# A recurrence's triangular inverse: substitution in 16-blocks, and one more block step on TensorE

## The chip, the cores and the metric

The program runs on one core of a Trainium2 chip. The core has five engines with queues of their own: TensorE (PE, matmuls), VectorE (DVE), ScalarE (ACT), GpSimd (POOL) and SyncE (SP, which here only issues DMAs). Each takes its instructions in the order written, and waits on semaphores for what it needs from the others. The metric is the device time of one execution in microseconds: 2445.03 us before, the median of 3 runs (2442.17 to 2445.43).

## The reference

Two layers of a diffusion backbone over 512 latent and 256 context tokens of width 1024. In each, three token mixers read one normalised input: a bidirectional RWKV-7 recurrence, a latent attention (MLA) and a windowed attention (GQA); their gated outputs are merged and projected. The change touches the recurrence alone:

```python
def step(S, inp):
    r_t, w_t, k_t, v_t, kk_t, a_t = inp
    sa = jnp.einsum('bhvk,bhk->bhv', S, kk_t)
    S = (S * w_t[:, :, None, :] - sa[..., None] * (kk_t * a_t)[:, :, None, :]
         + v_t[..., None] * k_t[:, :, None, :])
    return S, jnp.einsum('bhvk,bhk->bhv', S, r_t)
```

It runs over 768 steps for 8 heads of 64 channels, once in each direction, and all in float32.

## The kernel before, in words

The recurrence is not run step by step but in 12 chunks of 64 steps (`NCH`). Inside a chunk the steps depend on each other through a strictly triangular 64 x 64 matrix, one for each of the 16 pairs of head and direction; the kernel inverts one plus that matrix once and then needs matmuls alone. `zphase` computes the matrices on PE and leaves them in device memory (`tt_d`). `rwkv` works through the chunks: `rwkv_scores` loads a chunk's operands two chunks ahead and makes its score products (tiles `scps`, `AR`, `TR`, `bkp`), and `rwkv_step` makes the chunk's own chain: `Rp` (state and scores), `Up` (the inverse in `YB` times Rp), `Sp` (the new state `So`), and `Yp` (the output).

Inverses are made for four chunks at a time (`NS`, `NG` = 3 groups a layer), so there are six in the program. `rwkv_inverse` holds 64 matrices, in two 32 x 32 diagonal blocks each and one block off the diagonal. A 32-row strip of the 128 partitions holds one row of every block of its kind. The two kinds of diagonal blocks are inverted on DVE by substitution: for j from 30 to 1, a product of a column of the matrix and a row of the inverse (L630, j(31 - j) elements a partition), added to the rows above (L632). Three 32 x 32 transposes on DVE (L620 in front; L635 and L636 behind) turn the blocks as they are needed, and POOL's `affine_select` (L624) makes the start values. The block off the diagonal is then two matmul products on PE, `zp` (L645) and `yp` (L653), each in two halves of 16 matrices; these matmuls take 32 rows and 32 columns of the array, on two of its four strips in turn. ACT and DVE copy the results into `YB` (L648, L654, L655).

What sets the order. `band(b)` gives instructions a rank, and a scheduler fills each engine's queue by rank where dependencies allow it. The recurrence has rank `B + 1`. Fill work, the input projections that the attentions will need (tiles `g`, `st`; `wh` and `wl` are the high and low part of a weight, split by ACT in L165 and POOL in L166), has rank `B + 4`. `pace(n)` puts n steps of fill work there; a step is six matmuls in layer 0 (three over 512 columns and three over 256) and mostly three over 512 columns in layer 1. `in_line` adds an order for PE: every matmul of the recurrence from the end of the first inverse's substitution on is tied behind the one written before it. The fill between them counts too. So PE runs them exactly as written, and a matmul that waits holds all that follow.

```python
ahead = invert(0)
for _ in range(3):
    next(ahead)
...
pace(FILL[l][1])
...
    for _ in ahead:
        pace(FILL[l][2])
```

A generator's `yield` marks where the caller goes on with something else. The first inverse of a layer is driven by the lines above: substitution, `FILL[l][1]` steps of fill, then products with `FILL[l][2]` steps between. The inverses of the next groups are driven from the chunk loop, one `next(ahead)` behind each of the first three chunks of a group and up to three within the fourth; there the fill steps are `FILL[l][3]` and `FILL[l][4]`, 2 or 3 behind each part of a chunk.

Of the kernel before, what the change touches and what calls it, by code (L numbers as in the profile page):

```python
# [10 lines left out]
F32 = mybir.dt.float32  # L11
F32R = mybir.dt.float32r
BF16 = mybir.dt.bfloat16
AF = mybir.ActivationFunctionType
ALU = mybir.AluOpType
# [4 lines left out]
P = 128  # L20
# [9 lines left out]
GB, RB, CB = 2, 3, 2  # L30


FILL = ((48, 36, 2, (2, 2, 2), (3, 3, 3), 2), (72, 56, 4, (2, 2, 2), (3, 3, 3), 2))

QUEUES = (("scalar", "sync", "sync", "scalar"), ("sync", "scalar", "sync", "sync"))

# [1 line left out]
NS, NG = 4, 3  # L38
# [22 lines left out]
def build(tc, A, out):  # L61
    nc = tc.nc
    V, S, G, TE, DMA = nc.vector, nc.scalar, nc.gpsimd, nc.tensor, nc.sync
    weights = {}
    es = ExitStack()
    cpool = es.enter_context(tc.tile_pool(name="const", bufs=1))
# [3 lines left out]
    rps = es.enter_context(tc.tile_pool(name="rps", bufs=2, space=PSUM))  # L70
# [4 lines left out]
    @contextmanager  # L75
    def band(b):

        keep, mine = tc.cur_priority, bands.get(b, b * 1000000)
        tc.cur_priority = mine
        yield  # L80
        bands[b] = tc.cur_priority
        tc.cur_priority = keep
# [12 lines left out]
            DMA.dma_start(xs[k], A["xT"][:, k, :])  # L95
    C = {n: cst[:, o:o + w] for n, (o, w) in CC.items() if o < n_cst}
    ident, bones, ones = C["ident"], C["bones"], C["ones"]
    kbias = cpool.tile([P, 3], F32, name="kbias")
    V.memset(kbias[:, 0:1], EPS)
    V.memset(kbias[:, 1:2], GN_EPS)  # L100
    V.memset(kbias[:, 2:3], 10.0 * math.log(2.0))
    b_eps, b_gn, b_kk = kbias[:, 0:1], kbias[:, 1:2], kbias[:, 2:3]


# [35 lines left out]
    def queued(i):  # L140

        if line["on"] and line["last"] is not None:
            tc.add_manual_dep(i.ins, line["last"].name, mybir.DependencyInfo(
                mybir.DependencyClass.NoSync, mybir.DependencyReason.DATA), reason="line")
        line["last"] = i.ins

    @contextmanager
    def in_line():
        line["on"] = True
        yield  # L150
        line["on"] = False

    def mm(o, l, r, start=True, stop=True, **kw):
        queued(TE.matmul(o, l, r, start=start, stop=stop, **kw))  # L154
# [309 lines left out]
    def rwkv(l, D, last, DL, B, pace, zlast):  # L464

        with tc.tile_pool(name="rw", bufs=1, reuse_waits="tile") as rp:
            yo = rp.tile([P, 4, T], F32, name="yo")
            st = {"seen": set(), "S": None}
            parts, YB = {}, {}

            def scores(i):
                if i < NCH:
                    parts[i] = yield from rwkv_scores(l, last, rp, i)

            def invert(g):
                if g < NG:
                    YB[g] = rp.tile([P, 32, 64], F32, tag="YB", name="YB", bufs=2)
                    yield from rwkv_inverse(l, rp, g, YB[g])

            def rest(*gens):  # L480
                for g in gens:
                    for _ in g:
                        pass

            with band(B + 1):
                rest(scores(0), scores(1))
                ahead = invert(0)
                for _ in range(3):
                    next(ahead)
            with band(B + 4), tc.issue_after(zlast):  # L490
                pace(FILL[l][1])
            with band(B + 1), in_line():
                for _ in ahead:
                    pace(FILL[l][2])
                ahead = out = iter(())
                for i in range(NCH):
                    if i % NS == 0:
                        rest(ahead)
                        ahead = invert(i // NS + 1)
                    nxt = scores(i + 2)  # L500
                    step = rwkv_step(l, last, i, yo, st, DL, rp, parts.pop(i), YB[i // NS])
                    for n in FILL[l][3 if i % NS < NS - 1 else 4]:
                        next(step, None)
                        next(nxt, None)
                        if i % NS == NS - 1:
                            next(ahead, None)
                        next(out, None)
                        pace(n)
                    rest(step, nxt)
                    if i % NS < NS - 1:  # L510
                        next(ahead, None)
                    if i in READY and (i > 3 or not last):
                        rest(out)
                        out = readout(l, D, rp, yo, READY[i])
                for _ in out:
                    pace(FILL[l][5])

# [89 lines left out]

    def rwkv_inverse(l, rp, g, YB):

        TT = rp.tile([P, 8, NS, 64], F32, tag="TT", name="TT")  # L610
        cs = slice(g * NS, (g + 1) * NS)
        for b0 in (0, 64):

            DMA.dma_start(TT[b0:b0 + 32], tt_d[l][b0:b0 + 32, :, cs])
            DMA.dma_start(TT[b0 + 32:b0 + 64, :, :, 0:32], tt_d[l][b0 + 32:b0 + 64, :, cs, 32:64])
        inv = rp.tile([P, 1536], F32, tag="inv", name="inv")
        MB, tmp = inv[:, 0:1024], inv[:, 1024:1536]
        YK = YB[:, :, 32:64]
        TT4 = TT.rearrange("p c s t -> p (c s) t")
        V.transpose(MB, TT4[:, :, 0:32].rearrange("p n j -> p j n"))  # L620

        M3 = MB.rearrange("p (j i) -> p i j", i=32)
        Y3 = YK.rearrange("p j i -> p i j")
        G.affine_select(YK, MB.rearrange("p (j i) -> p j i", i=32),  # L624
                        [[1, 32], [-1, 32]], ALU.is_gt, 0.0, base=0, channel_multiplier=0)
        V.memset(YB.rearrange("p n c -> p (n c)")[:, 32:2048:65], 1.0)
        for j in range(30, 0, -1):
            n = 31 - j
            t3 = tmp[:, 256 * (j % 2):256 * (j % 2) + j * n].rearrange("p (i c) -> p i c", c=n)
            V.tensor_tensor(t3, M3[:, 0:j, j:j + 1].to_broadcast([P, j, n]),  # L630
                            Y3[:, j:j + 1, j + 1:32].to_broadcast([P, j, n]), ALU.mult)
            V.tensor_tensor(Y3[:, 0:j, j + 1:32], Y3[:, 0:j, j + 1:32], t3, ALU.add)  # L632
            if j in (22, 12):
                yield
        V.transpose(YB[:, :, 0:32].rearrange("p n j -> p j n"), YK)  # L635
        V.transpose(MB.rearrange("p (n j) -> p n j", j=32), YB[:, :, 0:32])  # L636
        for b0 in (32, 96):
            S.copy(YB[b0:b0 + 32, :, 32:64], YB[b0:b0 + 32, :, 0:32])
        X13 = MB.rearrange("p (n j) -> p n j", j=32)
        yield  # L640
        for n0 in range(0, 32, 16):
            zp = rps.tile([P, 16, 32], F32, tag="r", name="zp", bufs=RB)
            for n in range(16):
                for b0 in (0, 64):
                    mm(zp[b0 + 32:b0 + 64, n, :], TT4[b0:b0 + 32, n0 + n, 32:64], X13[b0:b0 + 32, n0 + n, :])  # L645
            z3 = tmp.rearrange("p (n j) -> p n j", j=32)
            for b0 in (32, 96):
                S.copy(z3[b0:b0 + 32], zp[b0:b0 + 32])  # L648
            yield
            yp = rps.tile([P, 16, 32], F32, tag="r", name="yp", bufs=RB)  # L650
            for n in range(16):
                for b0 in (0, 64):
                    mm(yp[b0:b0 + 32, n, :], z3[b0 + 32:b0 + 64, n, :], YB[b0 + 32:b0 + 64, n0 + n, 32:64])  # L653
            S.copy(YB[0:32, n0:n0 + 16, 32:64], yp[0:32])  # L654
            V.tensor_copy(YB[64:96, n0:n0 + 16, 32:64], yp[64:96])  # L655
        for b0 in (32, 96):
            G.memset(YB[b0:b0 + 32, :, 0:32], 0.0)
# [726 lines left out]
    for l in range(2):  # L1384
# [41 lines left out]
        def pace(n):  # L1426

            for _ in zip(range(n), steps):
                pass
# [3 lines left out]
        with band(B + 4):  # L1433
            pace(FILL[l][0])
        ss = cpool.tile([P, 6, 10], F32, tag="ss", name="ss")
        if last:
            cctx.close()
            with band(B + 3):
                gqa_tokens(l, F, last, ss)
        rwkv(l, D, last, DL, B, pace, zlast)  # L1440
        weights["queue"] = getattr(nc, QUEUES[l][2])
        with band(B + 4), tc.issue_after(line["last"]):
            pace(22 * 8 - sum(FILL[l][0:2]) - 2 * FILL[l][2] - NG * (3 * sum(FILL[l][3]) + sum(FILL[l][4])) - 4 * FILL[l][5])

        def gates():
            with band(B + 4):
# [160 lines left out]
```

## Time and profile before

| | before |
|---|---|
| median of 3 runs | 2445.03 us (2442.17 to 2445.43) |
| the profiled execution | 2438.52 us, span 2436.8 us |
| mean granted clock of PE | 0.947 |
| PE busy | 2190.0 us, 90% of the span |
| PE weight loads busy | 1667.8 us, 68% |
| DVE busy | 1276.0 us, 52% |
| ACT busy | 896.2 us, 37% |
| POOL busy | 849.6 us, 35% |

A span runs from the first to the last instruction of one execution. Busy times are shares of an engine's time in which some instruction of it ran; PE overlaps its matmuls, so their lengths add up to more than their starts are apart. The granted clock is 1.0 at 2.4 GHz and 0.5 at 1.2 GHz, and a mean over a stretch lies between. In a line of the timeline the number in brackets is the time in which the engine had nothing to run before that instruction, and what ended it. A float32 matmul leaves two records in the trace.

### The profile page before, as it was taken

What the parts mean: (1) busy time and instruction counts of PE and PEld (TensorE: products, weight loads), DVE (VectorE), ACT (ScalarE), POOL (GpSimd) and SP (SyncE); (2) the same over time, 40 slices, a digit from 0 to 9 for tenths busy, and PEclk for the clock granted to TensorE, in tenths of its full rate; (3) what the DMA queues carried; (4) which work ended last, traced back from release to release, by engine and by line L of the source; (5) the groups of instructions that cost most, each with busy time, mean ns of one, the idle gap of its engine ahead of it and who ended that gap; (6) DMA issues with size and microseconds to landing.
All of it is one profiled execution on the core that took longest, in us unless ns stands there. A gap on an engine that the chain in (4) does not pass through costs nothing. (4 is left out here: it accounts for less than half of the span.)

```text
span 2436.8 us, 42441 instructions
## 1 busy us (share of the span) xinstructions
PE 2190.0 (90%) x16652; PEld 1667.8 (68%) x16652; DVE 1276.0 (52%) x2282; ACT 896.2 (37%) x1658; POOL 849.6 (35%) x703
## 2 busy tenths in 40 slices
PE   7988897889999999899889997897878988999989
PEld 4765666767877667667668775686766766666667
DVE  5466336774357673365145447717776356545223
ACT  4443212233463333543212444422323454344322
POOL 1243321111133344443433235433211244454564
PEclk9999998999999999999989998898988989999989
DMA  7146664546331014312875215565643342021474
GB/s 250 61 137 206 187 175 123 138 119 154 121 130 54 29 41 141 124 46 69 255 225 182 96 64 162 173 186 158 142 108 83 108 140 91 14 61 31 148 266 147
DMA packets 322055, 313.62 MB, mean 129 GB/s; under 512 B 112768, under 2 KB 223104, under 8 KB 321856
## 3 DMA queue, kind: packets, MB, share of 16 engines
q1 hardware_dynamic: 306736, 283.38, 39.3%
q10 hardware_dynamic: 15120, 27.53, 3.5%
q8 instruction: 131, 2.15, 0.4%
q14 instruction: 68, 0.56, 0.1%
HBM read 213.05 MB, written 97.78 MB: 128 GB/s over the span
## 5 line engine op out<-in xcount | busy, mean ns | idle before, releaser
L166 POOL TENSOR_TENSOR wl<-wf,wh 128x512 fp32r<-128x512 f32 x320 | 431.2, 1350 | 1033.7 <-ACT wh L165 961.8
L154 PE MATMUL g<-hh,wh 128*128 128x512 f32 (+1 forms) x1296 | 482.2, 372 | 18.1 <-DVE st L730 15.2
L154 PE MATMUL g<-hh,wl 128*128 128x512 f32 (+1 forms) x1296 | 469.2, 362 | 0.8 <-POOL wl L166 0.8
L154 PE MATMUL g<-hl,wh 128*128 128x512 f32 (+1 forms) x1296 | 467.8, 361 | 0.0
L165 ACT CAST wh<-wf 128x512 fp32r<-128x512 f32 x320 | 197.4, 619 | 524.5 <-PE g L154 254.3
L154 PEld LDWEIGHTS g<-hh,wh 128*128 128x128 f32 x1296 | 256.2, 198 | 81.5 <-issue 22.3
L154 PEld LDWEIGHTS g<-hl,wh 128*128 128x128 f32 x1296 | 256.0, 198 | 41.5 <-issue 11.7
L154 PEld LDWEIGHTS g<-hh,wl 128*128 128x128 f32 x1296 | 256.4, 198 | 39.9 <-issue 5.9
L837 POOL TENSOR_TENSOR acc<-acc,pe 128x512 f32<-128x512 f32 (+2 forms) x128 | 146.1, 1141 | 155.0 <-ACT pe L833 142.3
L833 ACT ACTIVATE pe<-stp 128x256 f32<-128x256 f32 (+2 forms) x224 | 114.8, 522 | 207.3 <-PE stp L154 198.5
L815 DVE TENSOR_REDUCE mx<-mps 128x1 f32<-128x384 f32 (+2 forms) x256 | 127.6, 535 | 70.4 <-PE mps L154 68.2
L154 PE MATMUL yps<-pe,vh 128*64 128x256 f32 (+1 forms) x704 | 132.0, 385 | 0.0
L1317 DVE SCALAR_TENSOR_TENSOR zt<-zt,g 128x512 f32<-128x512 f32 (+1 forms) x56 | 31.9, 576 | 145.6 <-PE g L154 111.1
L154 PE MATMUL g<-yh,wh 128*128 128x512 f32 (+1 forms) x224 | 84.0, 382 | 22.4 <-ACT yh L1301 11.8
L632 DVE TENSOR_TENSOR YB<-YB,inv 128x30 f32<-128x30 f32 (+9 forms) x180 | 93.1, 517 | 5.1
L630 DVE TENSOR_TENSOR inv<-inv,YB 128x30 f32<-128x30 f32 (+9 forms) x180 | 89.8, 499 | 9.2 <-DMA BK<-bkd 3.0
L154 PE MATMUL g<-yl,wh 128*128 128x512 f32 (+1 forms) x224 | 84.6, 381 | 6.2 <-POOL yl L1302 6.2
L154 PE MATMUL gc<-hh,wh 128*128 128x512 f32 x192 | 79.2, 412 | 7.8 <-ACT hh L298 4.5
L154 PE MATMUL scps<-AR,BK 64*128 64x128 f32 (+1 forms) x768 | 65.8, 295 | 20.6 <-DVE TR L598 15.7
L596 DVE TENSOR_TENSOR AR<-scps,cst 64x256 f32<-64x256 f32 x96 | 40.1, 418 | 82.1 <-PE scps L154 80.9
L154 PE MATMUL g<-yh,wl 128*128 128x512 f32 (+1 forms) x224 | 82.2, 373 | 0.0
L728 ACT ACTIVATE st<-g 128x256 f32<-128x256 f32 (+1 forms) x108 | 56.6, 524 | 68.1 <-PE g L154 66.5
(389 smaller groups left out, 4387.8 us busy)
## 6 DMA issues: line engine op xcount, KB each, us to landing
wf<-w_in SPq DMA_DIRECT2D x159, 256.0 KB, 2.8
wf<-ada_w SPq DMA_DIRECT2D x96, 256.0 KB, 3.7
wf<-w_in ACTq DMA_DIRECT2D x81, 256.0 KB, 2.8
bkd<-bk SPq DMA_DIRECT2D x16, 768.0 KB, 5.3
zt<-thzg SPq DMA_DIRECT2D x48, 256.0 KB, 3.8
wf<-w_bo SPq DMA_DIRECT2D x40, 256.0 KB, 3.6
thzg<-st SPq DMA_DIRECT2D x24, 384.0 KB, 2.6
md<-zt SPq DMA_DIRECT2D x32, 256.0 KB, 3.7
```

The source lines that it names most:

```text
L154: queued(TE.matmul(o, l, r, start=start, stop=stop, **kw))
L165: S.copy(wh, w32)
L166: eng.tensor_tensor(wl, w32, wh.bitcast(F32), ALU.subtract)
L596: V.tensor_tensor(AR[oth, pds, 2 * par, :], ps[oth, :, a0:a0 + 64], msk("ms", oth), ALU.mult)
L630: V.tensor_tensor(t3, M3[:, 0:j, j:j + 1].to_broadcast([P, j, n]), Y3[:, j:j + 1, j + 1:32].to_broadcast([P, j, n]), ALU.mult)
L632: V.tensor_tensor(Y3[:, 0:j, j + 1:32], Y3[:, 0:j, j + 1:32], t3, ALU.add)
L728: S.activation(t[:, sl], p, AF.Tanh, scale=0.5)
L815: V.tensor_reduce(mx, ps, AX.X, ALU.max)
L833: S.activation(e, st, AF.Exp, scale=scale)
L837: G.tensor_tensor(acc, keep.pop(0, acc), e, ALU.add)
L1317: V.scalar_tensor_tensor(th, th, 1.0, p_, ALU.add, ALU.mult)
```

## The change

The 32 x 32 diagonal blocks are no longer inverted by substitution as a whole. Substitution runs in 16 x 16 blocks, for the two 16-blocks of a 32-block in one instruction (`both` is the view that holds them), for j from 14 to 1: 28 instructions over 2j(15 - j) elements. The 16-block off the diagonal is then made as the 32-block was: two matmul products on PE, `zq` and `yq`, 128 matmuls each, over 16 columns and on the four strips in turn. Between them ACT copies zq out with a scale that is 0 in the first 16 rows of a strip and 1 in the rest (`lower`); behind yq, ACT and DVE copy two strips each into YB, and one more transpose on DVE (L664 of the changed kernel) feeds the old zp. POOL clears the 16-block below the diagonal with a memset. The generator has its yields in other places: one behind the whole substitution, one behind zq, one behind yq and the last transpose; the number of parts is the same. The fill steps are set anew: 14 and 20 in front of the first inverse's products in place of 36 and 56, and 3 and 5 in each of now four places in place of 2 and 4 in two.

```diff
--- before.py
+++ after.py
@@ -30,7 +30,7 @@
 GB, RB, CB = 2, 3, 2
 
 
-FILL = ((48, 36, 2, (2, 2, 2), (3, 3, 3), 2), (72, 56, 4, (2, 2, 2), (3, 3, 3), 2))
+FILL = ((48, 14, 3, (2, 2, 2), (3, 3, 3), 2), (72, 20, 5, (2, 2, 2), (3, 3, 3), 2))
 
 QUEUES = (("scalar", "sync", "sync", "scalar"), ("sync", "scalar", "sync", "sync"))
 
@@ -95,10 +95,14 @@
             DMA.dma_start(xs[k], A["xT"][:, k, :])
     C = {n: cst[:, o:o + w] for n, (o, w) in CC.items() if o < n_cst}
     ident, bones, ones = C["ident"], C["bones"], C["ones"]
-    kbias = cpool.tile([P, 3], F32, name="kbias")
+    kbias = cpool.tile([P, 4], F32, name="kbias")
     V.memset(kbias[:, 0:1], EPS)
     V.memset(kbias[:, 1:2], GN_EPS)
     V.memset(kbias[:, 2:3], 10.0 * math.log(2.0))
+    lower = kbias[:, 3:4]
+    V.memset(lower, 1.0)
+    for q in range(0, P, 32):
+        V.memset(kbias[q:q + 16, 3:4], 0.0)
     b_eps, b_gn, b_kk = kbias[:, 0:1], kbias[:, 1:2], kbias[:, 2:3]
 
 
@@ -485,8 +489,7 @@
             with band(B + 1):
                 rest(scores(0), scores(1))
                 ahead = invert(0)
-                for _ in range(3):
-                    next(ahead)
+                next(ahead)
             with band(B + 4), tc.issue_after(zlast):
                 pace(FILL[l][1])
             with band(B + 1), in_line():
@@ -607,6 +610,7 @@
 
     def rwkv_inverse(l, rp, g, YB):
 
         TT = rp.tile([P, 8, NS, 64], F32, tag="TT", name="TT")
         cs = slice(g * NS, (g + 1) * NS)
         for b0 in (0, 64):
@@ -619,24 +623,47 @@
         TT4 = TT.rearrange("p c s t -> p (c s) t")
         V.transpose(MB, TT4[:, :, 0:32].rearrange("p n j -> p j n"))
 
-        M3 = MB.rearrange("p (j i) -> p i j", i=32)
-        Y3 = YK.rearrange("p j i -> p i j")
         G.affine_select(YK, MB.rearrange("p (j i) -> p j i", i=32),
                         [[1, 32], [-1, 32]], ALU.is_gt, 0.0, base=0, channel_multiplier=0)
+        G.memset(YK[:, 16:32, 0:16], 0.0)
         V.memset(YB.rearrange("p n c -> p (n c)")[:, 32:2048:65], 1.0)
-        for j in range(30, 0, -1):
-            n = 31 - j
-            t3 = tmp[:, 256 * (j % 2):256 * (j % 2) + j * n].rearrange("p (i c) -> p i c", c=n)
-            V.tensor_tensor(t3, M3[:, 0:j, j:j + 1].to_broadcast([P, j, n]),
-                            Y3[:, j:j + 1, j + 1:32].to_broadcast([P, j, n]), ALU.mult)
-            V.tensor_tensor(Y3[:, 0:j, j + 1:32], Y3[:, 0:j, j + 1:32], t3, ALU.add)
-            if j in (22, 12):
-                yield
+
+        def both(j0, nj, i0, ni):
+
+            return bass.AP(YK.tensor, YK.offset + 64 * j0 + i0, [YK.ap[0], [64 * 16 + 16, 2], [64, nj], [1, ni]])
+
+        for j in range(14, 0, -1):
+            n = 15 - j
+            t3 = tmp[:, 128 * (j % 2):128 * (j % 2) + 2 * j * n].rearrange("p (b c i) -> p b c i", b=2, c=n)
+            V.tensor_tensor(t3, both(j, 1, 0, j).to_broadcast([P, 2, n, j]),
+                            both(j + 1, n, j, 1).to_broadcast([P, 2, n, j]), ALU.mult)
+            V.tensor_tensor(both(j + 1, n, 0, j), both(j + 1, n, 0, j), t3, ALU.add)
+        yield
         V.transpose(YB[:, :, 0:32].rearrange("p n j -> p j n"), YK)
+        V.transpose(MB.rearrange("p (n j) -> p n j", j=32), YB[:, :, 0:32])
+        X13 = MB.rearrange("p (n j) -> p n j", j=32)
+
+        quads = [slice(b0, b0 + 32) for b0 in range(0, P, 32)]
+        zq = rps.tile([P, 32, 16], F32, tag="r", name="zq", bufs=RB)
+        for n in range(32):
+            for q in quads:
+                mm(zq[q, n, :], TT4[q, n, 0:32], X13[q, n, 0:16])
+        z3 = tmp.rearrange("p (n j) -> p n j", j=16)
+        S.activation(z3, zq, AF.Copy, scale=lower)
+        yield
+        yq = rps.tile([P, 32, 16], F32, tag="r", name="yq", bufs=RB)
+        for n in range(32):
+            for q in quads:
+                mm(yq[q.start:q.start + 16, n, :], z3[q, n, :], YB[q, n, 16:32])
+        for q in quads:
+            r = slice(q.start, q.start + 16)
+            if q.start < 64:
+                S.copy(YB[r, :, 16:32], yq[r])
+            else:
+                V.tensor_copy(YB[r, :, 16:32], yq[r])
         V.transpose(MB.rearrange("p (n j) -> p n j", j=32), YB[:, :, 0:32])
         for b0 in (32, 96):
             S.copy(YB[b0:b0 + 32, :, 32:64], YB[b0:b0 + 32, :, 0:32])
-        X13 = MB.rearrange("p (n j) -> p n j", j=32)
         yield
         for n0 in range(0, 32, 16):
             zp = rps.tile([P, 16, 32], F32, tag="r", name="zp", bufs=RB)
@@ -1440,7 +1467,7 @@
         rwkv(l, D, last, DL, B, pace, zlast)
         weights["queue"] = getattr(nc, QUEUES[l][2])
         with band(B + 4), tc.issue_after(line["last"]):
-            pace(22 * 8 - sum(FILL[l][0:2]) - 2 * FILL[l][2] - NG * (3 * sum(FILL[l][3]) + sum(FILL[l][4])) - 4 * FILL[l][5])
+            pace(22 * 8 - sum(FILL[l][0:2]) - 4 * FILL[l][2] - NG * (3 * sum(FILL[l][3]) + sum(FILL[l][4])) - 4 * FILL[l][5])
 
         def gates():
             with band(B + 4):
```

In the rows below a name is that of a tile, and x6 means that six such instructions follow one another. DVE at the start of layer 0's first inverse, before:

```order
L730 SCALAR_TENSOR_TENSOR st<-st,g 128x256
L241 TENSOR_TENSOR mod_162<-modpt,pp 128x2x4
L291 TENSOR_SCALAR gs<-mod_162 128x4
L292 TENSOR_TENSOR gs<-gs,pp 128x4
L730 SCALAR_TENSOR_TENSOR st<-st,g 128x512
L620 STREAM_TRANSPOSE inv<-TT 128x1024
L626 MEMSET YB 128x32
L630 TENSOR_TENSOR inv<-inv,YB 128x30
```

The same place after:

```order
L757 SCALAR_TENSOR_TENSOR st<-st,g 128x256
L624 STREAM_TRANSPOSE inv<-TT 128x1024
L638 TENSOR_TENSOR inv<-YB 128x28
L640 TENSOR_TENSOR YB<-YB,inv 128x2x14
L629 MEMSET YB 128x32
```

The three instructions on `mod`, which need a product of PE (modpt), and one st product now stand behind the inverse's transposes. On PE, the first product of layer 0's first inverse, before:

```order
L154 MATMUL g<-hh,wh 128x512
L154 MATMUL g<-hl,wh 128x512
L154 MATMUL g<-hh,wl 128x512
L154 MATMUL zp<-inv,TT 32x32 x32
L154 MATMUL modpt<-cst,row 128x2 x4
L154 MATMUL modps<-wf,sc_108 32x512 x2
```

And after:

```order
L158 MATMUL g<-hh,wh 128x512
L158 MATMUL g<-hl,wh 128x512
L158 MATMUL g<-hh,wl 128x512
L158 MATMUL zq<-inv,TT 32x16 x128
L158 MATMUL g<-hh,wh 128x512
```

Up to zq the rows of PE are the same as before; zq comes 134 rows earlier than zp did, since 22 steps of fill are no longer in front of it. On PE, ahead of the third chunk's Rp in layer 1, while the second inverse is made, before:

```order
L154 MATMUL g<-hl,wh 128x512
L154 MATMUL g<-hh,wl 128x512
L157 MATMUL gqm<-cst,raw 128x128 x2
L154 MATMUL Rp<-UV,AR 64x64 x16
L154 MATMUL scps<-AR,BK 128x128 x8
```

And after:

```order
L158 MATMUL g<-hl,wh 128x512
L158 MATMUL g<-hh,wl 128x512
L161 MATMUL gqm<-cst,raw 128x128 x3
L158 MATMUL zq<-inv,TT 32x16 x128
L158 MATMUL Rp<-UV,AR 64x64 x16
L158 MATMUL scps<-AR,BK 128x128 x8
```

Before, the first product of this inverse (zp) stood behind the fourth chunk's Rp; now zq stands ahead of the third's, and yq ahead of the fourth's.

## Rows read from the trace of the kernel before

**Rows 1.** The page's strip: PE's busy tenths in 40 slices.

```profile
PE   7988897889999999899889997897878988999989
```

**Rows 2.** Stretch, length, busy PE, PEld, DVE, ACT, POOL; granted clock, DMA, GB/s.

```profile
348.10:410.80 62.70, 49.13 (x452) 35.63 (x450) 42.35 (x80) 12.25 (x20) 11.39 (x9) 0.84 0.48 129
410.80:496.60 85.80, 78.55 (x1252) 63.87 (x1248) 60.00 (x124) 25.97 (x47) 13.01 (x11) 0.94 0.56 141
496.60:593.20 96.60, 85.52 (x1298) 67.61 (x1297) 62.27 (x135) 33.36 (x61) 11.12 (x10) 0.93 0.57 145
593.20:643.10 49.90, 49.64 (x717) 39.36 (x717) 18.91 (x41) 15.13 (x30) 7.68 (x6) 1.00 0.34 109
1664.80:1718.40 53.60, 40.24 (x387) 31.12 (x385) 36.60 (x63) 16.37 (x29) 16.95 (x14) 0.84 0.47 138
1718.40:1794.90 76.50, 58.43 (x924) 47.87 (x921) 57.34 (x118) 23.27 (x41) 13.47 (x12) 0.82 0.53 120
1794.90:1876.30 81.40, 66.84 (x1170) 54.83 (x1169) 59.56 (x117) 24.49 (x46) 11.71 (x10) 0.87 0.44 101
1876.30:1914.60 38.30, 38.30 (x641) 31.55 (x640) 16.52 (x36) 13.44 (x26) 5.60 (x5) 1.00 0.22 72
```

**Rows 3.** The page's groups: the substitution's 60 instructions in six inverses; busy, mean ns.

```profile
L632 DVE TENSOR_TENSOR YB<-YB,inv 128x30 f32<-128x30 f32 (+9 forms) x180 | 93.1, 517 | 5.1
L630 DVE TENSOR_TENSOR inv<-inv,YB 128x30 f32<-128x30 f32 (+9 forms) x180 | 89.8, 499 | 9.2 <-DMA BK<-bkd 3.0
```

**Rows 4.** Timeline of DVE, layer 0's first inverse: start, length, instruction, idle before.

```profile
355.64 0.15 DVE L630 TENSOR_TENSOR inv<-inv,YB 128x30 f32<-128x30 f32 x1 [1.41 <-issue]
...
357.61 1.30 DVE L632 TENSOR_TENSOR YB<-YB,inv 128x108 f32<-128x108 f32 x1
...
374.83 0.59 DVE L630 TENSOR_TENSOR inv<-inv,YB 128x240 f32<-128x240 f32 x1
...
391.12 1.89 DVE L635 STREAM_TRANSPOSE YB<-YB 128x1024 f32<-128x1024 f32 x1
393.05 1.25 DVE L636 STREAM_TRANSPOSE inv<-YB 128x1024 f32<-128x1024 f32 x1
```

**Rows 5.** Timeline of PE, layer 0's first inverse: the products.

```profile
394.35 1.92 PE L154 MATMUL zp<-inv,TT 32*32 32x32 f32 x64 [8.22 <-DVE inv L636]
...
405.28 0.22 PE L154 MATMUL zp<-inv,TT 32*32 32x32 f32 x2
...
405.37 1.11 PE L154 MATMUL zp<-inv,TT 32*32 32x32 f32 x59
...
409.65 1.20 PE L154 MATMUL yp<-YB,inv 32*32 32x32 f32 x64
```

**Rows 6.** Timeline at the start of layer 0's first inverse, DVE and PE.

```profile
348.00 0.42 DVE L730 SCALAR_TENSOR_TENSOR st<-st,g 128x256 f32<-128x256 f32 x1 [3.55 <-ACT st L728]
...
348.09 0.39 PE L154 MATMUL g<-hh,wh 128*128 128x512 f32 x1
...
352.20 2.03 DVE L620 STREAM_TRANSPOSE inv<-TT 128x1024 f32<-128x1024 f32 x1
```

**Rows 7.** Timeline in layer 1's first inverse, DVE and PE.

```profile
1649.66 2.04 DVE L620 STREAM_TRANSPOSE inv<-TT 128x1024 f32<-128x1024 f32 x1 [12.72 <-DMA TT<-ttd]
...
1670.35 0.80 PE L154 MATMUL g<-hh,wh 128*128 128x512 f32 x1 [5.20 <-DVE st L730]
```

**Rows 8.** Timeline: the later inverses' first transposes, and the chunks' Rp behind them.

```profile
422.11 2.00 DVE L620 STREAM_TRANSPOSE inv<-TT 128x1024 f32<-128x1024 f32 x1
...
442.42 1.40 PE L154 MATMUL Rp<-UV,AR 128*64 128x64 f32 x32 [0.58 <-ACT UV L667]
...
1728.15 2.03 DVE L620 STREAM_TRANSPOSE inv<-TT 128x1024 f32<-128x1024 f32 x1
...
1741.37 1.33 PE L154 MATMUL Rp<-UV,AR 128*64 128x64 f32 x32 [0.77 <-ACT UV L667]
...
1802.98 1.95 DVE L620 STREAM_TRANSPOSE inv<-TT 128x1024 f32<-128x1024 f32 x1
```

## The prediction

> **What bounds the kernel now.** I read the page's strip first: TensorE (PE) is at eight or nine tenths in most of the 40 slices of 61 us, and at seven in five, of which three (the 7th, 28th and 30th digits) lie in the recurrences of the two layers (348 to 650 us and 1665 to 1920 us) [rows 1]. Then I cut the recurrences into stretches at the first matmul of every fourth chunk (Rp) and asked for busy time and granted clock in each [rows 2]. A stretch that holds an inverse loses PE time in two ways: PE is idle, and after an idle time it runs at the lower of its two clock levels (1.2 GHz, granted 0.5) for some microseconds. The loss of a stretch is its length less PE busy, plus PE busy times one less the clock: 13.6 + 7.9 = 21.4 us in layer 0's first, then 12.0 and 17.1; in layer 1 19.8, 28.6 and 23.2. That is 122 us. The two stretches without an inverse lose 0.3 and 0 [rows 2]. So PE bounds the kernel, and the inverse is a main reason for which it stands still; VectorE (DVE) is busy 60.0 of 85.8 us in layer 0's second stretch, and 18.9 of 49.9 where there is no inverse [rows 2].
>
> Who is waited for: DVE. The 60 substitution instructions of an inverse take 182.9 us in six inverses, 30.5 each [rows 3]. In the first inverse they run from 355.64 to 391.12, and PE, out of fill work, waits 8.22 us for the last transpose [rows 4, 5].
>
> **What the change does to the sum.** Three things: DVE's part gets short, PE gets 256 matmuls an inverse, and less fill work stands in front of the first inverse.
>
> DVE. 28 instructions instead of 60. Their elements a partition are 2j(15 - j) for j from 1 to 14, twice: a mean of 80. An old product of 30 elements took 0.15 us and one of 240 took 0.59 [rows 4]; the line through both gives 0.255 at 80. With 0.04 between two, 28 take 8.4 us. Bounds: at the smallest row's 0.15, 5.3 us; at the old mean of 0.51 [rows 3], whatever the size, 15.4 us. I take 8.4, for the new operands run along neighbouring elements more often than the old ones. An instruction that meets GpSimd's wl (row 357.61: 108 elements in 1.30 us [rows 4]) costs 1 us more; I add one such meeting. The two old transposes (1.89 and 1.25) stay and one more of 1.25 comes, behind the yq copies. GpSimd's new memset is a quarter of the select's elements: 0.3 us by estimate.
>
> PE. A matmul of these shapes leaves two records. 2 x 128 matmuls in six inverses are 3072 records. The trace has no matmul on four 32-row strips in turn. On two strips, 64 yp records stand in a block of 1.20 us at full clock, the last of them 0.19 long: 16 ns a record [rows 5]. Where the last yp and the first zp overlap, so that all four strips are in use, 11 records start between 405.28 and 405.37: 8 ns [rows 5]. Bounds: 4 ns (four strips and half the columns) and 16 ns. I take 8: 256 records are 2.05 us, zq and yq together 4.1 us an inverse, 24.6 us in all.
>
> The Trainium skill speaks against this ("TensorE: Matmul & The Clock Gate", section "Wait — 56ns, not 53.3ns?"): matmuls start no closer than about 25 ns, however few columns they have. The trace does not agree with it across strips (16 ns on two), though 32 ns on one strip fits. By 25 ns a record the sum below would be 52 us worse.
>
> Fill. Fill steps in front of and inside the first inverse go from 36 + 2 x 2 to 14 + 4 x 3 in layer 0 and from 56 + 2 x 4 to 20 + 4 x 5 in layer 1. The 14 and 24 steps left out run after the recurrence, at PE's rate there; by my accounting of losses that costs nothing as long as PE has no idle time to lose there.
>
> The new wait. All PE work of this stretch keeps the order written, so at zq everything behind it waits, the chunk's Rp first.
> - Layer 0, first inverse. Up to zq, PE's order is the old one, and PE gets there at 348.1 [rows 6]. DVE no longer has three small mod instructions between the st product that ends at 348.42 and the load's transpose (row 352.20), so the chain starts 3.8 us earlier. From transpose to first substitution is 3.44 us (352.20 to 355.64, with GpSimd's select between) [rows 4, 6], plus 0.3 of memset: 352.2. Then 8.4 + 1.0 + 1.89 + 1.25 + 0.1: zq can start at 364.8. PE is idle 16.7 us, more than the old 13.6.
> - Layer 1, first. The transpose at 1649.66 waited for its load [rows 7], and I leave it there: + 3.7 + 8.4 + 2 meetings + 3.2 + 0.7 for an st product between the transposes, and 1.5 allowed for GpSimd coming late to the select, gives 1669. PE ran gap-free until 1670.35 - 5.20 = 1665.2 [rows 7]; with 12 fill matmuls fewer in front it arrives some 3 us earlier, at 1662. Wait: 7.
> - Layer 0, second. Transpose at 422.11 [rows 8]; to the second new transpose it is 2.0 + 1.7 + 12.6 of its own and 6.3 of a step's other DVE work (18.9 / 3 in the clean stretch [rows 2]): 444.7. PE gets to the place of zq, just ahead of the third Rp, at 442.42 - 0.58 = 441.8 [rows 8]. Wait: 2.9.
> - Layer 1, second: 1728.15 + 22.6 = 1750.8 against 1741.37 - 0.77 = 1740.6 [rows 8], plus a transpose for the tokens in front. Wait: 9.5. Third: 1802.98 + 22.6 = 1825.6 against two clean steps of 12.8 after 1794.9 [rows 2, 8]: 1820.5. Wait: 5.
> - Layer 0, third: its steps take 20 us, so zq is ready first. I leave 3 us of old waits for loads.
> After such a wait PE runs at half clock for a while (block 394.35: 1.92 us for what takes 1.20 at full clock [rows 5]): I lose 3 us after 7 or more, 1.5 to 2 after less.
>
> The sum, old loss less new wait, clock, and 4.1 for PE, and 1 us a stretch for small waits:
> layer 0: 21.4 - 16.7 - 3 - 4.1 - 1 = -3.4; 12.0 - 2.9 - 1.5 - 4.1 - 1 = 2.5; 17.1 - 3 - 4.1 - 1 = 9.0.
> layer 1: 19.8 - 7 - 3 - 4.1 - 1 - 2 (a token transpose that PE waits for in this stretch, left as it is) = 2.7; 28.6 - 9.5 - 3 - 4.1 - 1 = 11.0; 23.2 - 5 - 2 - 4.1 - 1 = 11.1.
> Together 33 us. The profiled execution took 2438.5 us (span 2436.8), so the same one would take 2405.5. The runs' median is 2445.0, 6.5 above; I take the gain from it: 2412.
>
> **The rivals.**
> Packing stops at two strips. Small matmuls then cost what yp's do: 16 ns, and twice the array's time at half clock (zp's 64 records spread over 1.92 - 0.19 us: 27 ns) in the five zq that follow a wait. At 16 throughout the added PE time doubles and some 8.5 us of gain is left: 2436. With 27 at five zq it is 14 us worse: 2450, slower. The place is zq and yq on PE; it decides against the change from 33 / 3072 = 10.7 ns above mine, some 19 ns a record. For it: no matmul before is on four strips in turn. Against it: the 8 ns at the overlap.
>
> A floor under every record. If a record started 25 ns after the one before on whatever strip, 3072 x 17 ns = 52 us more would end at 2464. This is the Trainium skill's rule cited above; the trace's 16 ns leaves it little room.
>
> The substitution stays dear. If an instruction costs 0.51 us whatever its size, because short inner runs (1 to 14 elements in four dimensions) cost more than elements, five of the six zq come 7 us later: the gain is gone, and one more meeting with GpSimd in each makes it 2450. Against it: the size rule holds from 30 to 240 elements.
>
> zq's waits are smaller. At 5.3 us for 28 and no meetings, each of four waits shrinks by 4 us and their slow clock with them: some 25 us more, 2387.
>
> Nothing comes of it: the 38 fill steps, out of idle time before, run in places that had no room, and small matmuls' waits eat the rest: 2441 to 2449.
>
> **How the numbers follow.** Forecast as worked out (2398 to 2426): 0.50. Two strips at 16 ns: 0.12; with half clock: 0.06; the floor: 0.02. Dear substitution: 0.10. Smaller waits: 0.13. Nothing: 0.07. 0.2% of 2445 is 4.9 us, about what a measurement of this kernel can tell from no change. Faster by more (under 2440.1): 0.50 + 0.13 + 0.09 of the 16 ns case = 0.72. Within: 0.03 of that case, 0.06 of nothing and 0.03 of the dear one = 0.12. Slower: the remaining 0.16. The range goes from the case of smaller waits to the edge of the slower cases: 2384 to 2447.
>
> **What would show it.** In the profile after: the 28 instructions at a mean near 0.25 us; 256 records each of zq and yq in about 2.1 us; a wait of PE of about 17 us for the second transpose ahead of the first zq, and of 3 to 10 ahead of three or four others; the waits for st products in layer 1 gone; PE's loss in the second and third stretches of layer 1 about halved. Wrong would be: zq or yq over 4 us, substitution over 12 us of DVE time, waits at zq above 20 us, or a recurrence that ends earlier by as much as I say while the span does not shorten, for then the fill steps were paid for later.

## The result, and the profile after

The changed kernel took 2461.02 us (median of 20 runs, 2447.03 to 2470.08), the kernel before, beside it, 2442.27 (20 runs, 2433.96 to 2448.78): a ratio of 1.0082, 95% interval 1.0070 to 1.0095. That is 19 us slower, where I had forecast 33 us faster. The profiled execution has a span of 2453.4 us against 2436.8; TensorE (PE) is busy 2205.4 us instead of 2190.0, and idle as long as before (248.0 us, 246.8 before).

The stretches that answer to [rows 2], cut at the first Rp of the same chunks and begun where PE first stops for the inverse (columns as in [rows 2]):

```profile
347.40:397.90 50.50, 31.28 (x860) 24.78 (x860) 17.42 (x43) 9.62 (x15) 5.99 (x6) 0.76 0.46 107
397.90:492.80 94.90, 83.20 (x1765) 67.93 (x1758) 44.37 (x100) 27.84 (x50) 13.62 (x12) 0.91 0.45 119
492.80:602.50 109.70, 94.77 (x1816) 76.73 (x1815) 48.14 (x108) 35.97 (x65) 11.74 (x10) 0.88 0.49 125
602.50:651.30 48.80, 48.54 (x720) 39.64 (x718) 17.47 (x38) 14.66 (x28) 6.39 (x5) 1.00 0.34 108
1678.90:1720.20 41.30, 29.12 (x828) 24.08 (x828) 11.83 (x20) 11.98 (x19) 8.82 (x8) 0.79 0.38 103
1720.20:1798.50 78.30, 63.69 (x1440) 52.89 (x1432) 41.43 (x89) 25.43 (x47) 13.12 (x12) 0.85 0.53 122
1798.50:1883.60 85.10, 70.94 (x1686) 59.09 (x1685) 41.98 (x93) 26.96 (x51) 12.43 (x12) 0.88 0.46 108
1883.60:1921.90 38.30, 38.30 (x643) 31.54 (x642) 17.82 (x38) 13.47 (x26) 5.50 (x5) 1.00 0.24 71
```

DVE got its relief (layer 0's second stretch: 44.37 us busy instead of 60.00). But the losses, reckoned as in the prediction, are 26.7, 19.2 and 26.3 us in layer 0 and 18.3, 24.2 and 22.7 in layer 1: 137 us, where 122 stood before and 65 was forecast. What PE waits for now stands in the waits of the whole span (engine, tile, line, what it waited for; us in total, times, longest):

```profile
PE zq L158 <- issue: 38.5, 9, 14.4
...
PE yq L158 <- issue: 14.6, 7, 3.5
```

"issue" means that nothing in the profile is seen to release the instruction. Two of the zq waits, 14.40 us in layer 0's and 7.65 in layer 1's first inverse, end just after the transpose that zq needs, and are waits for DVE. The others stand in the middle of a run of matmuls that all have their operands. Layer 0's second inverse (start, length, instruction, count, idle before):

```profile
436.01 2.04 PE L158 MATMUL zq<-inv,TT 32*32 32x16 f32 x223
440.91 0.44 PE L158 MATMUL zq<-inv,TT 32*32 32x16 f32 x33 [2.86 <-issue]
441.28 1.03 PE L158 MATMUL Rp<-UV,AR 128*64 128x64 f32 x16
```

```profile
458.92 1.11 PE L158 MATMUL yq<-YB,inv 32*16 32x16 f32 x103
460.62 1.30 PE L158 MATMUL yq<-YB,inv 32*16 32x16 f32 x128 [0.59 <-issue]
464.90 0.36 PE L158 MATMUL yq<-YB,inv 32*16 32x16 f32 x25 [2.98 <-issue]
465.19 1.12 PE L158 MATMUL Rp<-UV,AR 128*64 128x64 f32 x16
```

Read the counts: between the two pauses of yq lie exactly 128 records. Each record has a weight load beside it, so that is 256 instructions. The page's DMA queues say what comes in such pieces, first before, then after (packets, MB, share):

```profile
q8 instruction: 131, 2.15, 0.4%
```

```profile
q8 instruction: 155, 2.54, 0.4%
```

24 packets more for 2 x 3072 instructions more: one packet of 0.39 MB / 24 = 16 KB is a page of 256 instructions, and PE is fed its program by DMA. The two traces hold 131.6 and 155.7 times 256 instructions of PE, weight loads and waits on semaphores included, as many as the queue has packets. The pause of 2.86 us ended at 440.91; the DMA rows of 438.0 to 439.4 us hold one such packet:

```profile
q8 instruction: 1, 0.02, 5.0%
```

I counted PE's instructions from the start of the program. In the two recurrences 16 idle times over 0.3 us in or just behind zq and yq (four of over 3 us, the longest 4.57) end where that count stands at the same place in a page (193 or 194 above a multiple of 256), each 2.3 to 2.8 us after such a packet began. They sum to 38.7 us. Before, there was one of them, 0.55 us inside yp.

### The profile page after: what moved, and what is told of

The parts are those of the page before. It is cut to its first block, busy times and chain, and to the rows that moved or that the text cites. A ratio compares the mean times of both kernels' runs of the same rounds, so it can differ in the third digit from the quotient of the medians.

```text
span 2453.4 us, 48446 instructions
## 1 busy us (share of the span) xinstructions
PE 2205.4 (90%) x19724; PEld 1691.9 (69%) x19724; DVE 1170.6 (48%) x2113; ACT 906.0 (37%) x1676; POOL 848.4 (35%) x709
## 5 line engine op out<-in xcount | busy, mean ns | idle before, releaser
L158 PE MATMUL g<-hh,wh 128*128 128x512 f32 (+1 forms) x1296 | 476.4, 368 | 2.7 <-ACT hh L302 2.1
L158 PE MATMUL gc<-hl,wh 128*128 128x512 f32 x192 | 79.4, 414 | 0.0
L158 PE MATMUL gc<-hh,wl 128*128 128x512 f32 x192 | 77.3, 402 | 0.0
L158 PEld LDWEIGHTS yps<-pe,vh 128*64 128x64 f32 x704 | 53.1, 135 | 34.4 <-issue 21.3
```

## The experiments

Medians of the runs (20 of the first two kernels, 4 to 10 of each other), the ratio to the kernel before on the same chip, the page pauses in the recurrences (in one profiled execution: idle times of PE over 0.3 us that end at that place of the count, wherever they stand), the length from the last chunk's Rp of layer 1 to the end, and the fill steps in front of and inside the recurrences (layer 0, layer 1):

| kernel | us | ratio (95%) | page pauses, us | last stage, us | fill steps |
|---|---|---|---|---|---|
| before | 2442.27 | 1 | 0.6 | 522.2 | 177, 225 |
| changed | 2461.02 | 1.0082 (1.0070 to 1.0095) | 38.7 | 531.5 | 163, 201 |
| grouped (e1) | 2410.0 | 0.9866 (0.9849 to 0.9882) | 6.4 | 488.2 | 181, 237 |
| no zq, yq (e2b) | 2410.2 | 0.9870 (0.9841 to 0.9899) | 0 | 537.4 | 163, 201 |
| fill behind (e6) | 2448.7 | 1.0029 (1.0014 to 1.0044) | 32.9 | 495.3 | 181, 237 |
| grouped, no fill added (e8) | 2431.1 | 0.9961 (0.9937 to 0.9984) | 5.7 | 528.6 | 163, 201 |
| cover (e4) | 2466.1 | 1.0089 (1.0060 to 1.0119) | 34.8 | 529.5 | 177, 209 |
| grouped and cover (e5) | 2425.0 | 0.9925 (0.9900 to 0.9950) | 5.2 | 485.7 | 191, 245 |
| before, more fill (e3) | 2410.0 | 0.9876 (0.9862 to 0.9891) | 0 | 488.8 | 181, 237 |
| before, 12 in layer 1 (e9) | 2409.6 | 0.9876 (0.9840 to 0.9912) | 1.1 | 486.5 | 177, 237 |
| changed, 12 in layer 1 (e10) | 2457.2 | 1.0064 (1.0039 to 1.0088) | 34.0 | 518.3 | 163, 213 |
| c1 | 2411.0 | 0.9875 (0.9841 to 0.9909) | 1.4 | 487.7 | 181, 249 |
| c2 | 2408.7 | 0.9865 (0.9833 to 0.9897) | 8.9 | 486.6 | 163, 237 |

Theory A says that PE waits for its own instructions. Its rivals: B, every small matmul costs some 20 ns wherever it stands; C, the loss is the wait for DVE ahead of zq and the fill missing there; D, the pages are late only through other DMA traffic; and, once the groups had worked, E, that they worked through more fill in the recurrences.

**The products alone (m1).** A program that runs only matmuls of zq's shape: 1024 on four strips; 1024 on one; 1024 on four with four 128x512 matmuls after every 32; 1024 on four beside weight loads. Forty matmuls of 128x512 stand ahead of each part. It ran once.

> A program of its own, none of the reference's work: 1024 matmuls of zq's shape on four strips in a row with no DMA beside them, 1024 on one strip, 1024 in groups of 32 with four 128x512 matmuls behind each group, and 1024 on four strips beside 32 MB of weight loads. Theory A: on four strips records start 8 to 9 ns apart in blocks of 128, with a pause at each page, 3 to 4.5 us from page to page; on one strip 32 ns a record and no pause; hardly any in the mixed part. Whether the loads make the pauses longer tells contention (rival D: no pauses without DMA beside) from a fixed time of fetching. Rival B: records evenly 20 to 25 ns apart, without pauses.

PE's timeline, the first rows of each part (sa, sb, mx with ml, sd):

```profile
17.59 1.71 PE L79 MATMUL sa<-x,w 32*32 32x16 f32 x183
21.52 1.75 PE L79 MATMUL sa<-x,w 32*32 32x16 f32 x128 [2.22 <-issue]
24.97 1.90 PE L79 MATMUL sa<-x,w 32*32 32x16 f32 x128 [1.71 <-issue]
...
84.12 107.69 PE L79 MATMUL sb<-x,w 32*32 32x16 f32 x2048
...
202.95 0.73 PE L79 MATMUL mx<-x,w 32*32 32x16 f32 x64
203.61 1.20 PE L79 MATMUL ml<-xr,wr 128*128 128x512 f32 x4
204.73 0.73 PE L79 MATMUL mx<-x,w 32*32 32x16 f32 x64
...
274.23 1.77 PE L79 MATMUL sd<-y,w 32*32 32x16 f32 x190
280.67 1.91 PE L79 MATMUL sd<-y,w 32*32 32x16 f32 x128 [4.67 <-issue]
286.87 1.90 PE L79 MATMUL sd<-y,w 32*32 32x16 f32 x128 [4.29 <-issue]
```

The expectation of theory A held. On four strips, blocks of 128 records follow one another every 3.5 to 4.0 us with nothing else on the DMA queues, and every 6.2 to 6.5 us while the loads ran. The profile's strip of that program (40 slices of 9.3 us) shows both, the granted clock and the loads:

```profile
PEclk9965555586555555555559998999995555555555
...
GB/s 85 0 5 5 4 5 4 5 2 2 2 4 2 2 4 2 2 4 2 4 2 0 5 4 5 4 5 4 73 412 408 406 408 408 409 406 409 295 5 225
```

So a page has a time of its own, and other transfers lengthen it: rival D is half right. Inside a block, at the lower of the two clock levels (0.5, 1.2 GHz), 128 records take 1.90 us. On one strip 2048 records run through, 52.6 ns each at the lower clock; I had put 32, twice the 16 ns that yp's records took on two strips at the full clock. With long matmuls between the groups (a page in about 3.4 us) three pauses of 0.58 to 0.99 us were left in 62 us.

**Groups with fill between (e1).** The same matmuls, written in four groups each, with one fill step between two groups in layer 0 and two in layer 1. That adds 18 and 36 steps to the recurrences, which are then missing at the end. For zq (cut to the loop; yq's is changed in the same way):

```diff
 for n in range(32):
     for q in quads:
         mm(zq[q, n, :], TT4[q, n, 0:32], X13[q, n, 0:16])
+    if n % 8 == 7 and n < 31:
+        pace((1, 1, 1)[n // 8] * (1 + l))
```

> The changed kernel with each zq and each yq written in four groups of 32 matmuls, and one fill step (two in layer 1) between groups; the same matmuls and the same fill in all. Theory A (the pauses inside zq and yq are TensorE waiting for its own instructions, fetched in pages of 256): long matmuls between the groups give the fetch time, the 16 pauses (38.7 us) shrink to under 10 us and the slow clock behind them goes: 2410 to 2425 us. Rival B (each small matmul costs some 20 ns wherever it stands): nothing changes, 2455 to 2465. Rival C (the loss is the wait for DVE ahead of the first zq, and fill that is missing there): nothing changes either.

2410.0 us. The pauses fell to 6.4 us, and rivals B and C with them: the small matmuls do not cost their time wherever they stand.

**The control (e6): the same added fill, but behind each unbroken batch.** For zq (a cut; the same line stands behind yq):

```diff
                 mm(zq[q, n, :], TT4[q, n, 0:32], X13[q, n, 0:16])
+        pace(3 * (1 + l))
```

> The control for the run with the groups: the same 18 and 36 extra fill steps in the recurrences, but all three (six in layer 1) behind each unbroken zq and yq instead of between groups of 32. Theory A: the pauses stay inside zq and yq, 30 us or more, and the time stays at 2440 to 2460. If the gain of the grouped kernel came from more fill in the recurrences, not from the spacing (rival E): 2410 to 2418.

2448.7 us with 32.9 us of pauses. Between e6 and e1 only the place of the fill differs, and that is 39 us in the medians (35 between the two profiled executions). The six stretches with an inverse, cut as above, first of e6, then of e1 (columns as in [rows 2]):

```profile
346.50:404.60 58.10, 39.51 (x897) 30.41 (x897) 18.79 (x46) 12.37 (x20) 9.80 (x9) 0.77 0.49 119
404.60:506.50 101.90, 92.69 (x1819) 73.90 (x1813) 44.79 (x101) 28.14 (x51) 12.45 (x11) 0.95 0.48 122
506.50:612.40 105.90, 95.84 (x1857) 77.22 (x1856) 47.15 (x107) 36.95 (x67) 13.52 (x12) 0.97 0.56 142
1680.80:1730.00 49.20, 37.26 (x864) 30.88 (x864) 13.20 (x22) 14.37 (x23) 12.69 (x11) 0.79 0.39 107
1730.00:1817.50 87.50, 71.64 (x1472) 58.37 (x1465) 41.08 (x86) 27.77 (x50) 15.65 (x14) 0.86 0.53 128
1817.50:1909.80 92.30, 81.90 (x1720) 67.46 (x1719) 40.13 (x87) 29.67 (x54) 15.79 (x14) 0.89 0.41 97
```

```profile
351.60:406.20 54.60, 38.44 (x900) 28.64 (x899) 18.93 (x46) 12.47 (x20) 9.86 (x9) 0.84 0.55 128
406.20:502.70 96.50, 90.03 (x1819) 71.50 (x1815) 44.69 (x101) 28.23 (x51) 12.55 (x11) 1.00 0.50 129
502.70:604.00 101.30, 95.44 (x1855) 76.12 (x1854) 47.27 (x107) 37.48 (x67) 13.93 (x12) 0.98 0.58 148
1666.60:1711.30 44.70, 35.77 (x866) 28.09 (x865) 13.85 (x24) 14.96 (x25) 12.64 (x11) 0.89 0.50 131
1711.30:1794.10 82.80, 71.55 (x1479) 57.37 (x1471) 43.12 (x92) 28.04 (x51) 17.36 (x16) 0.90 0.57 136
1794.10:1881.90 87.80, 79.83 (x1724) 64.53 (x1723) 42.06 (x91) 29.96 (x55) 16.99 (x15) 0.94 0.44 105
```

They take 494.9 us in e6 and 467.7 in e1: PE is idle 20 us less and busy 8 us less, and the granted clock is higher in every stretch. Another 7 us lie in the last stage (495.3 and 488.2).

**Grouped without added fill (e8).** As e1, with the chunk steps' FILL lowered to (2, 2, 1), (2, 2, 2) and (1, 2, 1), (1, 1, 1).

> The grouped kernel with no fill added: the 6 and 12 steps that stand between the groups of an inverse are taken from the chunk steps of the same four chunks, so that each recurrence holds as much fill as in the changed kernel. Theory A: against the changed kernel only the pauses and their slow clock go, 39 us or more: 2415 to 2425, and the last stage keeps its 530 us. Rival E (more fill in the recurrences made the grouped kernel fast): 2445 or more.

2431.1 us: 30 us below the changed kernel, not 36 to 46, and below the kernel before. The added fill was therefore part of e1's gain, though not the larger. The same place in layer 0's second inverse reads:

```profile
431.75 0.72 PE L158 MATMUL zq<-inv,TT 32*32 32x16 f32 x64 [0.62 <-DVE inv L643]
432.40 0.50 PE L158 MATMUL g<-hh,wh 128*128 128x512 f32 x1
...
433.76 0.81 PE L158 MATMUL zq<-inv,TT 32*32 32x16 f32 x64
...
435.63 0.68 PE L158 MATMUL zq<-inv,TT 32*32 32x16 f32 x58
437.14 0.24 PE L158 MATMUL zq<-inv,TT 32*32 32x16 f32 x6 [0.83 <-issue]
...
439.56 0.73 PE L158 MATMUL zq<-inv,TT 32*32 32x16 f32 x64
```

**Without the products (e2b).** One matmul of 128x512 in the place of each batch of 128.

> The changed kernel with the 128 zq matmuls of an inverse replaced by a single one over the whole tile, and the 128 of yq likewise (the inverse's lower blocks are then not computed). It prices all of the added TensorE work with the substitution as changed. Theory A (pages of instructions): products, pauses and the slow clock behind them go, some 65 to 75 us off the changed kernel: 2385 to 2397. If the loss is not in zq and yq (rival C): 2432 to 2440.

2410.2: all of zq and yq cost 51 us net, less than the 65 to 75 expected. The waits for the transposes stayed (25.5 us at zq), and the two records that replace a batch took up to 2 us.

**More fill ahead of the first inverse (e4, and grouped e5).** FILL's second number 28 and 28, then 24 and 28.

> The changed kernel with 28 fill steps ahead of the first inverse in both layers instead of 14 and 20. The waits of 14.4 and 7.65 us ahead of the first zq close; theory A expects just these and the slow clock behind them: 2435 to 2442, with the pauses inside zq and yq left at 35 us or more. Rival C (the waits ahead of zq are the main loss): 2420 or less.

> The grouped kernel with 24 and 28 fill steps ahead of the first inverse instead of 14 and 20, against the waits of 14.4 and 7.65 us ahead of the first zq. Theory A, with the pauses gone: the waits' cover is worth 5 to 12 us here, 2398 to 2405; by the run with 28 steps, which gained nothing, it is 2408 to 2412.

Both missed: e4 gained nothing, and e5 is 15 us slower than e1. In e4's first inverse of layer 0 the wait ahead of zq shrank from 14.4 to 5.1 us and changed its name (the zq and yq lines are page pauses):

```profile
PE g L158 <- DVE st L757: 3.8, 1, 3.8
PE zq L158 <- issue: 1.9, 1, 1.9
PE yq L158 <- issue: 1.9, 1, 1.9
PE g L158 <- ACT wh L169: 1.3, 1, 1.3
```

The added fill needs its st product from DVE, which is in the substitution. Why the 9 us saved there do not shorten e4 is open, and so is why e5 also takes 13 us more than e1 between the fourth and the eighth chunk of layer 0.

**Fill in the kernel before (e3, e9) and in the changed one (e10).** FILL's third number 4 and 10 (e3), 2 and 10 (e9); in the changed kernel 3 and 8 (e10).

> The kernel before with 4 more fill steps in layer 0's first inverse and 12 more in layer 1's, about as many in front of and inside the recurrences as the grouped kernel has. Rival E: some 15 us faster or more, 2425. Theory A: the kernel before has no long run of small matmuls, so this gives at most a few us: 2434 to 2444.

> The kernel before with 12 more fill steps in layer 1's first inverse alone. If what gained 30 us before (4 and 12 more steps) is the end of the program, whose order changes with the fill left for it: 2410 to 2416, and a last stage of some 488 us instead of 522. If it is the cover of the waits in the first inverses: half of it or less, 2425 or more.

> The changed kernel with 12 more fill steps in layer 1's first inverse (32 then stand ahead of zp instead of 20). If each 12 steps move as much from the end of the program as in the kernel before, 2430 to 2436; if only the step from 225 to 237 steps in layer 1 does it (here it is 201 to 213), 2452 to 2464. The pauses stay in both.

e3 refuted what I expected of it: 16 fill steps moved gain the kernel before 30 us, and e9 shows that the 12 of layer 1 are enough. The gain lies after the last chunk. The last stage of the kernel before, then of e9 (columns as in [rows 2]):

```profile
1914.60:2436.80 522.20, 477.01 (x2445) 343.81 (x2444) 230.34 (x437) 208.01 (x389) 247.03 (x199) 0.95 0.35 114
```

```profile
1918.50:2405.00 486.50, 456.99 (x2409) 328.44 (x2408) 232.48 (x437) 204.61 (x384) 240.65 (x196) 0.98 0.38 120
```

36 matmuls fewer, some 8 us at 0.23 each, but 36 us less time and a higher clock: with 237 steps of layer 1 behind it, the end of the program runs with fewer waits. From 201 to 213 steps (e10) the stage shortened by 13 us, from 225 to 237 by 36. What in the order of the end does that was not tried.

**Two more (c1: grouped with 249 steps in layer 1; c2: layer 0 as in e8, layer 1 as in e1).**

> The grouped kernel with 12 more fill steps in layer 1's first inverse (249 in layer 1 instead of 237). If more fill taken from the end of the program goes on paying, 2400 to 2406; if the step from 225 to 237 was all, 2406 to 2414.

> Grouped as before, with layer 0's fill as in the run that adds none (6 steps taken from the chunk steps) and layer 1's as in the grouped kernel (237 steps). Layer 0's recurrence has then no extra fill: theory A with the end of the program as the other term gives 2405 to 2414 again, the 21 us between the two grouped kernels lying in layer 1's fill; if layer 0's fill made the difference, 2425 or more.

2411.0 and 2408.7: more steps do not pay further, and c2 shows that the 21 us between e8 and e1 lie in layer 1's fill. e1, e3, e9, c1 and c2 all beat both kernels by over 1%, and are the same within their intervals. So with equal fill in layer 1 (237 steps) the old inverse (e9) and the new one in groups (c2) take the same time, with 177 and 163 steps in layer 0: once the end of the program is in its better order, splitting the substitution is worth nothing that these runs can tell.

## Why the prediction was wrong

- **DVE.** Right. The substitution, row by row (min, median, max ns):

```profile
L638 DVE TENSOR_TENSOR inv<-YB x84: 151/250/1244, 350.7 to 1820.8; 128x28 f32<-128x28 f32 x12, 128x52 f32<-128x52 f32 x12, 128x72 f32<-128x72 f32 x12, 128x88 f32<-128x88 f32 x12
```

  The median is 0.250 us where I had 0.255 [rows 4], and layer 0's first substitution runs 7.7 us, from 350.72 to 358.46 (8.4 and 1.0 forecast; 28 times 0.295 is 8.3, a slip that changes nothing). The rival of the dear substitution is out.
- **The waits at zq.** Right in kind, too long in sum: 14.4 us (16.7 forecast) and 7.65 (7) in the first inverses; in the others 0, 0, 3.3 and 0 (2.9, 0, 9.5 and 5). Waits that the forecast lacks, at modps (4.4) and scps (5.0 and 2.8), stand in the same stretches instead.
- **Packing.** Right as a rate: in layer 0's first inverse 124 yq records stand in 1.19 us, the last 0.17 long, at full clock: 8.3 ns. The rival of two strips is out.

```profile
373.81 1.19 PE L158 MATMUL yq<-YB,inv 32*16 32x16 f32 x124
```

- **The step that failed: "256 records are 2.05 us, zq and yq together 4.1 us an inverse, 24.6 us in all."** I took a rate from 11 records [rows 5] and let 512 instructions run at it. Only once did PE run all 256 records of a batch without a break (yq in layer 1's first inverse, in 2.41 us), and then it stopped for 2.89 us four matmuls behind them; in the other eleven batches it stopped inside. From one pause to the next it got 256 instructions in 3.5 us or more. The batches without their pauses took 35.7 us, part of them at the lower clock, and the pauses 38.7: 74 us instead of 24.6. That e6 and e1 differ as they do shows that the pauses, and not the matmuls themselves, were the loss.
- **A second term that was too small: the slow clock.** By the prediction's own accounting the six stretches lose 137 us where 65 were forecast. Of the 72 between, 38.7 are the pauses, and 38 are the lower clock: I allowed 12.5 us for it, and the rows above give 50.5 (44.2 before). The other idle time, 48 us, is about the 52 forecast. In e6 the same reckoning gives 43.5, and in e1, with the same fill and 6.4 us of pauses left, 23.9: much of the clock's loss comes with the pauses, but what is left without them is still twice my 12.5. The reckoning is rough: between e6 and e1 it falls by 39 us in all, while the stretches shorten by 27.
- **What is chance.** The span is 50 us over the one that the forecast meant (2436.8 - 33 = 2403.8, against 2453.4), and the products cost 50 us more than forecast. That the two agree is luck: the lower clock in the rest of the stretches comes on top, and against it stand mainly the fill steps left for later, which cost less than their own time (below).
- **The floor of 25 ns.** Its 2464 was near the measured 2461, but for another reason: 74 us over 3072 records are 24 ns as a mean, but inside a block they stand 8.3 ns apart at the full clock and about 13 at the lower one, and then PE has nothing for microseconds. Had it been a floor, e1 and e8 could not have moved the time with as many records. So the Trainium skill's rule cited in the prediction came near the size of the loss here by chance. The page "Runtime: NRT & Kernel Launch" of the Trainium skill (section "Instruction fetch mechanics") says that the instruction memory is refilled in blocks of 256 instructions and that this is mostly hidden, since instructions are issued more slowly than they come. The block agrees with the 128 records between pauses; the hiding does not hold for these matmuls (a block used in 1.2 to 1.9 us, refilled in 3.5 to 6.5).
- **Fill left for later.** Right for the steps that were moved: the stretch between the layers got 81 matmuls more and is 5.9 us longer (1027.6 after 1021.7), the last stage 76 more and 9.3 us longer, less than their own time. What I had not seen is that the last stage can be 36 us shorter with 36 matmuls less.
- **My own sign of error** ("zq or yq over 4 us") named the right place: zq in layer 0's second inverse takes from 436.01 to 441.28.

## What to carry to other kernels

Ask of every run of short instructions not only how fast the engine does them but how fast it is given them: here a page of 256 TensorE instructions takes 3.5 us alone and over 6 beside heavy loads, and each of the twelve runs of two pages at 8 to 15 ns a record met a pause, eleven of them before their end. Write long matmuls between groups of short ones (64 records with one fill step in layer 0 and two in layer 1 left 6.4 us of 38.7). Pauses with no releaser in a run of ready instructions, a fixed number of instructions apart, are the mark of it; and before an edit is credited with a gain, run the old kernel with the same fill.

## What was not expected of the hardware

- A page of instructions: 3.5 to 4.0 us from one to the next with idle DMA queues, 6.2 to 6.5 beside 406 to 412 GB/s of loads, 2.3 to 2.8 us from the start of its packet to the first matmul of the page in the changed kernel.
- Short matmuls with such pauses between them do not hold the clock: after the first slices m1's strip shows 0.5 (1.2 GHz) through the part on four strips, and again on one strip, where PE is never idle; behind forty long matmuls, and with four of them after every 64 records, it stays at 0.8 to 0.9.
